# A float32 decoder layer on one core: the order at the joints, the rotary's engine, and where evictions stand

## The chip, the cores and the metric

The kernel runs on one core of a Trainium2 chip. The metric is the device time of one execution in microseconds (us). A core has a matrix engine (TensorE, PE in the rows; PEld is its weight load), VectorE (DVE), ScalarE (ACT), GpSimd (POOL) and SyncE (SP), which here issues the loads. The TensorE clock has two levels, 1.2 and 2.4 GHz; the rows give the granted clock of a stretch as a share of the higher one.

## The reference

One layer on 256 tokens of width 2048, in float32, with an RMS norm before and after each part:

```python
f = swiglu(rmsnorm(x, ffn1_pre_g), ffn1_w_gate, ffn1_w_up, ffn1_w_down)      # 2048 -> 5632 -> 2048
x = x + 0.5 * rmsnorm(f, ffn1_post_g)
proj = rmsnorm(x, mix_pre_g) @ w_in                                          # q, k, v of two groups of 8 heads
o_a = moba_attention(partial_rope(q_a), partial_rope(k_a), v_a)              # rotary on 32 of 128 dimensions
o_b = stick_breaking_attention(q_b, k_b, v_b)
o = concat([rmsnorm(o_a, moba_out_g), rmsnorm(o_b, sb_out_g)])
x = x + rmsnorm(o @ w_out, mix_post_g)
f = swiglu(rmsnorm(x, ffn2_pre_g), ffn2_w_gate, ffn2_w_up, ffn2_w_down)
x = x + 0.5 * rmsnorm(f, ffn2_post_g)
```

With 256 tokens MoBA has one block, so its attention is plain causal softmax.

## The kernel before

The program runs through three parts: FFN 1 (tiles named f1, or f), the mixing part (mix) and FFN 2 (f2). The residual x lies in `xn`, 128 tokens on the partitions, two token tiles t = 0, 1 and four column chunks c of 512.

**Weights.** All weights are streamed from HBM once, in blocks of up to 1 MB, on SP's queue, into three raw buffers (`Weights.RAW`). A block is cut into pieces of 128x1024 numbers. ScalarE casts each piece to a hi part (`whi`, L142), VectorE subtracts that to get the lo part (`wlo`, L147), and TensorE multiplies hi by the activations' hi and lo parts and lo by their hi part, summed in PSUM. `split_next` does the cast and returns the subtraction as a function; `PARTS` = 4 pairs of parts exist beside those that a joint takes from the general slots.

**Block products.** Some pairs of weight rows go through sums (a seven-product scheme: `add_sums` L103 to L111 makes the sums in the raw buffer, in two steps around the casts), the others are plain. `HALVES` and `OUT` give the order of the pairs for w_down and w_out. Each has two column blocks u = 0, 1. Behind the last pair with sums the products are joined (`joins`, L740 to L745), spread over the steps that follow; `later(n, f)` puts f behind the n-th next piece. At the end of a block each bank is added to its row (`finish`, `join` L750), `Post.take` squares it on ScalarE (L388) and multiplies it by the gain row on VectorE (L660).

**Joints.** Where one part ends and the next begins, `Rows.tail` keeps the last three pairs back and runs them bank by bank: `mm(t, c)` is one bank of the tail, in the order (0,0), (0,1), (1,0), (1,1). `handover.end` writes by hand the order of all four compute engines (`ordered`): the bank's sum L750, the square, the gain L660, `column` (the rstd of one tile: L396 and L397 before the last square, L399, L375, L376 and three rounds of L371 and L372 behind it), the update of xn (L651), and `Pre.turn`: TensorE transposes xn (L479), ScalarE writes the hi part of the normed activations xg (L445), VectorE the lo part (L446). `take_over` then multiplies the first four pieces (`AHEAD`) of the next weights for tile 0, turns tile 1 and multiplies them for tile 1. Elsewhere the scheduler of the language sets the order of each engine.

**The mixing part.** `project_qk` makes q and k of two heads at a time. `put_qk` adds the two halves of a product (L632), multiplies by the norm's factor R (L1107), and for the group with rotary shuffles 32 rows (L1110) and does three steps on GpSimd: times the sine table (L1111), times the cosine table (L1112), added (L1113). The scores (`sp`, L1142) come a step or two later. `norm(g, start)` places the norms of the attention's output in the steps of what follows; its last part makes the pairs o0 to o7 for the product with w_out (o0 and o6 with sums, L671 to L677).

## Time and profile before

| | |
|---|---|
| time, median of three runs | 1872.8 us (1872.69 to 1872.9) |
| profiled execution | 1871.75 us, span 1870.0 us |
| TensorE busy | 1828.5 us, 98% of the span |
| VectorE busy | 1573.6 us, 84% |
| ScalarE busy | 1034.5 us, 55% |
| GpSimd busy | 86.7 us, 5% |
| mean granted TensorE clock | 0.992 |
| moved by DMA | 359.91 MB, mean 192 GB/s |

Joint 1 (FFN 1 to the mix) lies at 707 to 747 us, the rotary heads at 898 to 999, joint 2 (mix to FFN 2) at 1111 to 1158, and the last boundary between two column blocks at 1805 to 1823. All times in the rows are counted from the start of the span, of one execution; the seconds of an engine that nobody waits for cost nothing.

### The profile page before, as it was taken

The page shows a single profiled execution, that of the slowest core. Times are in us where ns is not written, and L with a number is a line of the kernel's source. Part 1 is how long each engine was busy: PE and PEld are TensorE (multiplying, and loading weights), DVE is VectorE, ACT ScalarE, POOL GpSimd, SP SyncE. Part 2 cuts the span into 40 slices and gives each one's busy share as a digit, 9 for nine tenths or more (in the row PEclk, how much of TensorE's full clock was granted, in tenths as well). Part 3 has the DMA queues.
Part 4 walks back from the last instruction along what each step waited for, and adds up shares of the span by engine and source line. Part 5 has one row for each costly group of instructions (what it writes and reads, how often), then busy time and mean ns, then how long its engine had stood idle before and what let it go on. Part 6 is the DMA issues. An engine that isn't in the chain of part 4 may idle for free.

```text
span 1870.0 us, 23366 instructions
## 1 busy us (share of the span) xinstructions
PE 1828.5 (98%) x8586; PEld 1519.7 (81%) x8586; DVE 1573.6 (84%) x2181; ACT 1034.5 (55%) x1388; POOL 86.7 (5%) x96
## 2 busy tenths in 40 slices
PE   9999999999999998999989997999999999999997
PEld 8888888888888876888878786788888888888876
DVE  6999998769999988556885786999999668999988
ACT  7655555545565554655545554765555445555553
POOL 0000000000000000000453100000000000000000
PEclk9999999999999999999999998999999999999999
DMA  8466555555655745554445455555555465555753
GB/s 269 150 209 210 200 192 203 185 198 183 210 203 205 259 169 186 187 180 158 158 144 171 170 194 169 169 188 204 201 195 215 175 224 181 199 205 194 252 197 136
DMA packets 181859, 359.91 MB, mean 192 GB/s; under 512 B 8880, under 2 KB 58224, under 8 KB 181744
## 3 DMA queue, kind: packets, MB, share of 16 engines
q1 hardware_dynamic: 179360, 351.31, 54.1%
q0 software_dynamic: 2208, 7.04, 1.1%
q8 instruction: 67, 1.10, 0.2%
q14 instruction: 48, 0.39, 0.1%
q10 hardware_dynamic: 176, 0.07, 0.0%
HBM read 354.19 MB, written 4.19 MB: 192 GB/s over the span
## 4 chain that ended last, share of the span: by engine, by line
PE 86%; DVE 9%; ACT 2%; issue 1%; DMA 1%; POOL 1%; DVEq 0%; ACTq 0%; SPq 0%
PE b L698 36%; PE d L698 17%; PE b_X L698 7%; PE pq L516 5%; PE d_X L698 4%; PE pv L535 4%; DVE wlo L147 3%; PE pq L525 3%; PE p L516 2%; PE w L698 2%; PE p L525 1%; PE ht L958 1%; ACT whi L142 1%; PE w_X L698 1%; ACT sqd L388 1%
## 5 line engine op out<-in xcount | busy, mean ns | idle before, releaser
L142 ACT CAST whi<-raw 128x1024 fp32r<-128x1024 f32 (+1 forms) x833 | 816.5, 1005 | 700.3 <-DVE raw L106 175.7
L147 DVE TENSOR_TENSOR wlo<-raw,whi 128x1024 fp32r<-128x1024 f32 (+1 forms) x833 | 952.0, 1169 | 241.8 <-ACT whi L142 235.8
L698 PE MATMUL b<-whi,x 128*128 128x512 f32 x1200 | 370.0, 389 | 0.0
L698 PEld LDWEIGHTS b<-whi,x 128*128 128x128 f32 x1200 | 225.1, 188 | 46.9
L698 PE MATMUL d<-whi,h 128*128 128x512 f32 x768 | 237.4, 389 | 0.4 <-ACT whi L142 0.4
L698 PE MATMUL b<-wlo,x 128*128 128x512 f32 x600 | 203.3, 389 | 0.2
L698 PEld LDWEIGHTS d<-whi,h 128*128 128x128 f32 x768 | 144.0, 188 | 31.1 <-ACT whi L142 1.3
L698 PE MATMUL b_X<-whi,x 128*128 128x512 f32 x400 | 155.8, 390 | 0.0
L516 PE MATMUL pq<-xg_mix,whi 128*128 128x512 f32 x512 | 133.6, 403 | 0.0
L698 PEld LDWEIGHTS b<-wlo,x 128*128 128x128 f32 x600 | 112.5, 188 | 24.5 <-DVE wlo L147 1.1
L698 PE MATMUL d<-wlo,h 128*128 128x512 f32 x384 | 130.6, 389 | 0.0
L516 PEld LDWEIGHTS pq<-xg_mix,whi 128*128 128x128 f32 x512 | 93.3, 191 | 17.3
L698 PE MATMUL d_X<-whi,h 128*128 128x512 f32 x256 | 99.3, 393 | 0.0
L698 PEld LDWEIGHTS b_X<-whi,x 128*128 128x128 f32 x400 | 75.1, 188 | 16.0 <-DVE x L446 0.4
L698 PEld LDWEIGHTS d<-wlo,h 128*128 128x128 f32 x384 | 72.0, 188 | 15.1
L535 PE MATMUL pv<-whi,xg_mix 128*128 128x512 f32 x256 | 82.7, 395 | 0.6 <-DVE xg_mix L446 0.6
L698 PE MATMUL b_X<-wlo,x 128*128 128x512 f32 x200 | 77.8, 389 | 0.0
L525 PEld LDWEIGHTS pq<-xg_mix,wlo 128*128 128x128 f32 x512 | 70.3, 191 | 5.4
L525 PE MATMUL pq<-xg_mix,wlo 128*128 128x256 f32 x512 | 71.7, 283 | 0.0
L111 DVE TENSOR_TENSOR raw<-raw 128x512 f32<-128x512 f32 x88 | 61.3, 697 | 2.0
L110 DVE TENSOR_TENSOR raw<-raw 128x512 f32<-128x512 f32 x88 | 60.8, 691 | 2.0
L106 DVE TENSOR_TENSOR raw<-raw 128x512 f32<-128x512 f32 x88 | 61.0, 693 | 1.6
(326 smaller groups left out, 2650.5 us busy)
## 6 DMA issues: line engine op xcount, KB each, us to landing
raw<-in_ffn_w_down_dram SPq DMA_DIRECT2D x86, 1024.0 KB, 5.0
raw<-in_ffn_w_up_dram SPq DMA_DIRECT2D x168, 512.0 KB, 4.7
raw<-in_ffn_w_gate_dram SPq DMA_DIRECT2D x167, 512.0 KB, 3.7
raw<-in_w_in_dram SPq DMA_DIRECT2D x48, 1024.0 KB, 5.1
raw<-in_w_out_dram SPq DMA_DIRECT2D x15, 1024.0 KB, 4.9
raw<-in_ffn_w_gate_dram SPq DMA_DIRECT2D x4, 1024.0 KB, 5.5
raw<-in_ffn_w_up_dram SPq DMA_DIRECT2D x4, 1024.0 KB, 5.0
xn<-in_x_dram SPq DMA_DIRECT2D x8, 256.0 KB, 6.2
```

The source lines that it names most:

```text
L106: eng.tensor_sub(q[:, 1], q[:, 3], q[:, 1])
L110: eng.tensor_add(q[:, 3], q[:, 3], q[:, 0])
L111: eng.tensor_sub(q[:, 2], q[:, 2], q[:, 3])
L142: self.nc.scalar.copy(hi, raw)
L147: self.nc.vector.tensor_sub(lo, raw, hi.bitcast(F32))
L388: nc.scalar.activation(d, src, AF.Square, accum_out=self.ss[:, t, c:c + 1])
L516: nc.tensor.matmul(p, wh, x, start=k == 0, stop=False)
L525: nc.tensor.matmul(p[:, :T], lo[:, j, f * P:(f + 1) * P], xs(k)[:, 0, :], start=False, stop=k == KD - 1)
L535: nc.tensor.matmul(ps[c], y, w[:, j, c * CH:(c + 1) * CH], start=first and n == 0, stop=last and n == 2)
L698: nc.tensor.matmul(self.ps[x], y, w, start=m == 1, stop=m == self.n[x])
L958: nc.tensor.transpose(p4[:, 2 * j + t], tg[2 * t + 1][:, k * P:(k + 1) * P], ident)
```

## The change

Five things are edited.

1. In `handover` and `take_over`, the four pieces that come next are no longer split in front of the tail's first sum. Their casts come behind the second sum of tile 0. The four lo parts (`lows`) come one behind the gain multiplication of tile 1's first sum and three in `take_over`. The V products of pieces 1 to 3 with tile 0 that need a lo part are done with tile 1's. The updates of xn in chunks 2 and 3 are moved into `take_over`.
2. The first gate and up weights of FFN 2 are loaded as blocks of both matrices, two pieces a block, in place of one block of half the size for each piece.
3. The rotary's cosine table gets ones in the rows without rotary, both tables are multiplied once by R, and all steps of the rotary are on VectorE.
4. The last column block of w_out takes its pairs in the order 4, 6, 5, 0, 7 in place of 4, 5, 6, 7, 0, and the norm of the rotary group starts a step later.
5. The gain multiplications L660 leave `Post.take`. At the boundary between two column blocks they come with steps 7, 8, 13 and 14 of the next block; in the joints and at the end they have places of their own.

```diff
     cos, sin = np.cos(ang), np.sin(ang)
+    m[:, M_COS:M_COS + T] = 1
     m[:ROT, M_COS:M_COS + T] = np.concatenate([cos, cos])
...
-OUT = ((4, 5, 6, 7, 0), (6, 0), (1, 2, 3))
+OUT = (((4, 5, 6, 7, 0), (4, 6, 5, 0, 7)), (6, 0), (1, 2, 3))
...
             c0 = fp * 2 * P
-            if fp == 0:
+            if fp == 0 and n == 1:
                 plan["gu", n, fp] = []
...
                         ]
+            elif fp == 0:
+                plan["gu", n, fp] = [
+                    (None, 4 * c + 2 * s, i) for c in range(4)
+                    for s, i in enumerate(W.add((wg, wu), 4 * c, 4, c0, 4 * P))
+                ]
             else:
...
-    def take_over(pre, mm, ids):
+    def take_over(pre, first, second, ids):
+
         parts = [W.get(ids[m], 0) for m in range(AHEAD)]
+        lows = pre.lows
         for m in range(AHEAD):
-            mm(m, parts[m], 0)
-        W.split_next()()
+            first(m, parts[m], m == 0)
+        more = W.split_next()
         his, los = pre.turn(0, (1,))
         run_all(his)
+        pre.update(1, 1)
         run_all(los)
+        lows[1]()
         his, los = pre.turn(1, (1,))
         run_all(his)
-        mm(0, parts[0], 1)
+        second(0, parts[0], True)
+        lows[2]()
         run_all(los)
+        pre.update(2, 0)
         pre.update(2, 1)
-        mm(1, parts[1], 1)
-        W.split_next()()
+        second(1, parts[1], False)
+        lows[3]()
+        more()
+        second(2, parts[2], False)
+        his, los = pre.turn(2)
+        run_all(his)
+        more = W.split_next()
+        pre.update(3, 0)
+        run_all(los)
+        second(3, parts[3], False)
         pre.update(3, 1)
-        mm(2, parts[2], 1)
-        pre.group(2)
-        mm(3, parts[3], 1)
+        more()
         slots.give(*W.kept)
...
             ordered()
-            for m in range(AHEAD):
-                W.split_next(slots.take)()
             mm(0, 0)
...
             run_all(before)
+            post.finish()
             mm(0, 1)
             finish(1, 0)
+            lows = [W.split_next(slots.take) for _ in range(AHEAD)]
             post.finish()
...
             pre = make()
+            pre.lows = lows
             pre.update(0, 0)
...
             run_all(before)
+            post.finish()
+            lows[0]()
             run_all(los)
...
             pre.update(0, 1)
-            pre.update(1, 1)
-            pre.update(2, 0)
-            pre.update(3, 0)
         return end
...
             self.late.append(((c, t), lambda: nc.vector.tensor_mul(dst, src, self.rows.chunk(c))))
-            if c < NC - 1:
-                self.finish()
...
                     self.finish(c, t)
+                if self.last:
+                    for n in (7, 8, 13, 14):
+                        later(n, lambda: self.post.finish(1))
...
                 W.split_to(i + 1)
-                if j == 1 and k0 + nk < KD:
+                if j != 0 and (k0 + nk) % 4 == 0 and k0 + nk < KD:
                     mm(m, (hi, lo, 1))
...
             def banks(j):
+                if j is None:
+                    return banks(0) + banks(1)
                 if j not in ps:
...
-    cosv = rots[:ROT, :T]
+    cosv = rots[:, :T]
...
-        def mm(m, part, ts):
-            for t in ts:
-                if t not in pv:
-                    pv[t] = bank(f"pv{g}{half}{t}")
-                for terms in ((0, 1), (2,)):
-                    for j in range(part[2]):
-                        k = ids[m][0] + j
-                        mm_tok([pv[t]], part, j, pre.x(k), t, k == 0, k == KD - 1, terms)
+        def mm(m, part, t, groups=((0, 1), (2,))):
+            if t not in pv:
+                pv[t] = bank(f"pv{g}{half}{t}")
+            for terms in groups:
+                for j in range(part[2]):
+                    k = ids[m][0] + j
+                    mm_tok([pv[t]], part, j, pre.x(k), t, k == 0, k == KD - 1, terms)
+
+        def second(m, part, whole):
+            if not whole:
+                mm(m, part, 0, ((1,),))
+            mm(m, part, 1)
...
             rest = AHEAD
-            take_over(pre, lambda m, part, t: mm(m, part, (t,)), [i for _, i in ids])
+            take_over(pre, lambda m, part, whole: mm(m, part, 0, ((0, 1), (2,)) if whole else ((0,), (2,))), second,
+                      [i for _, i in ids])
         for m in range(rest, len(ids)):
             part = W.get(ids[m][1])
-            mm(m, part, (0,))
+            mm(m, part, 0)
             if rest and m == 5:
                 pre.group(3)
-            mm(m, part, (1,))
+            mm(m, part, 1)
             step()
...
             later(0, pre.spread)
+            later(3, lambda: nc.vector.tensor_mul(cosv, cosv, pre.R))
+            later(4, lambda: nc.vector.tensor_mul(sinv, sinv, pre.R[:ROT]))
         vts[g, half] = slots.take([P, NT, 512], F32, f"vt{g}{half}")
...
             q = qk(g, h)[:, j, :]
-            nc.vector.tensor_mul(q, s, pre.R)
+            nc.vector.tensor_mul(q, s, cosv if g == 0 else pre.R)
             if g == 0:
                 sh = tmp.tile([ROT, T], F32, tag="right", name="sh")
-                nc.vector.stream_shuffle(sh, q[:ROT], swap)
-                nc.gpsimd.tensor_mul(sh, sh, sinv)
-                nc.gpsimd.tensor_mul(q[:ROT], q[:ROT], cosv)
-                nc.gpsimd.tensor_add(q[:ROT], q[:ROT], sh)
+                nc.vector.stream_shuffle(sh, s[:ROT], swap)
+                nc.vector.tensor_mul(sh, sh, sinv)
+                nc.vector.tensor_add(q[:ROT], q[:ROT], sh)
         return run
...
             later(f // (1 + half), outs[4 * half + f])
-    norm(0, 2)
+    norm(0, 3)
...
                 run_all(before)
+                post.finish()
                 if t:
```

**Place 1: VectorE in joint 1.** Names: wlo349 to wlo352 are the lo parts of the four next pieces (V weights of the mix), d111_2 and d111_3 the tail's banks for tile 0, fg_f12 and fg_f13 the output rows. Before, from the tail's third own lo part (wlo348) on:

```order
L147 TENSOR_TENSOR wlo348_5901<-raw136_5864,whi348_5900 128x1024
L147 TENSOR_TENSOR wlo349_5909<-raw137_5888,whi349_5908 128x1024
L147 TENSOR_TENSOR wlo350_5913<-raw137_5888,whi350_5912 128x1024
L147 TENSOR_TENSOR wlo351_5919<-raw138_5898,whi351_5918 128x1024
L147 TENSOR_TENSOR wlo352_5923<-raw138_5898,whi352_5922 128x1024
L750 TENSOR_TENSOR fg_f12_2528<-d111_2_5614,fg_f12_2528 128x512
L660 TENSOR_TENSOR fg_f12_2528<-fg_f12_2528,r_ffn1_post_g1_5179 128x512
L396 TENSOR_REDUCE rs_post_f10_5948<-ssq_post_f1_2530 128x1
L397 TENSOR_SCALAR rs_post_f10_5948<-rs_post_f10_5948 128x1
L750 TENSOR_TENSOR fg_f13_2529<-d111_3_5616,fg_f13_2529 128x512
```

After, from the same row on (the line numbers are those of the changed file: L148 is the lo part, L766 the sum, L678 the gain, L402 to L382 the rstd):

```order
L148 TENSOR_TENSOR wlo348_5901<-raw136_5864,whi348_5900 128x1024
L766 TENSOR_TENSOR fg_f12_2528<-d111_2_5610,fg_f12_2528 128x512
L402 TENSOR_REDUCE rs_post_f10_5927<-ssq_post_f1_2530 128x1
L403 TENSOR_SCALAR rs_post_f10_5927<-rs_post_f10_5927 128x1
L678 TENSOR_TENSOR fg_f12_2528<-fg_f12_2528,r_ffn1_post_g1_5179 128x512
L766 TENSOR_TENSOR fg_f13_2529<-d111_3_5612,fg_f13_2529 128x512
L678 TENSOR_TENSOR fg_f14_5952<-fg_f13_2529,r_ffn1_post_g1_5179 128x512
L405 TENSOR_SCALAR rs_post_f10_5927<-ssq_post_f1_2530,rs_post_f10_5927 128x1
L381 TENSOR_SCALAR rs_post_f10_5927<-rs_post_f10_5927 128x1
L382 TENSOR_SCALAR rs_post_f10_5927<-rs_post_f10_5927 128x1
L377 TENSOR_SCALAR rs_post_f10_5927<-rs_post_f10_5927 128x1
L378 SCALAR_TENSOR_TENSOR rs_post_f10_5927<-rs_post_f10_5927 128x1
```

The four lo parts wlo349 to wlo352 stood between the tail's own lo part and the first sum; now the sum follows at once. And a little further on after the change, from tile 1's first sum (d111_4) on:

```order
L766 TENSOR_TENSOR fg_f12_2528<-d111_4_5618,fg_f12_2528 128x512
L402 TENSOR_REDUCE rs_post_f11_6027<-ssq_post_f1_2530 128x1
L403 TENSOR_SCALAR rs_post_f11_6027<-rs_post_f11_6027 128x1
L678 TENSOR_TENSOR fg_f12_2528<-fg_f12_2528,r_ffn1_post_g1_5179 128x512
L148 TENSOR_TENSOR wlo349_5956<-raw137_5888,whi349_5955 128x1024
L452 SCALAR_TENSOR_TENSOR xg_mix0_5997<-xt_mix00_6014,G_97,xg_mix0_5997 128x128 x2
L452 SCALAR_TENSOR_TENSOR xg_mix1_5998<-xt_mix01_6017,G_97,xg_mix1_5998 128x128 x2
L452 SCALAR_TENSOR_TENSOR xg_mix2_5999<-xt_mix10_6042,G_97,xg_mix2_5999 128x128 x2
L452 SCALAR_TENSOR_TENSOR xg_mix3_6000<-xt_mix11_6045,G_97,xg_mix3_6000 128x128 x2
```

Here one of the four lo parts, wlo349, now stands between the gain of tile 1's first sum and the four lo parts of xg (L452, L446 before); the other three stand behind tile 1's transposes.

**Place 2: VectorE in the rotary, the second pair of heads.** pq0110 and pq0111 are the banks of k of heads 2 and 3, g their sums, qk01 the result that `sp2` and `sp3` need. Before:

```order
L632 TENSOR_TENSOR g_7962<-pq0110_7801,right_7960 128x256
L673 TENSOR_TENSOR or6_7958<-or6_7958 128x128
L1107 TENSOR_TENSOR qk01_7832<-g_7962,R_mix_6359 128x256
L674 TENSOR_TENSOR or6_7958<-or6_7958 128x128
L1110 STREAM_SHUFFLE sh_7965<-qk01_7832 32x256
L147 TENSOR_TENSOR wlo417_7983<-raw171_7849,whi417_7982 128x1024
L632 TENSOR_TENSOR g_7972<-pq0111_7802,right_7970 128x256
L677 TENSOR_TENSOR o6l_8008<-or6_7958,o6h_8007 128x896
L1107 TENSOR_TENSOR qk01_7832<-g_7972,R_mix_6359 128x256
L147 TENSOR_TENSOR wlo418_8012<-raw171_7849,whi418_8011 128x1024
L1110 STREAM_SHUFFLE sh_7975<-qk01_7832 32x256
```

After (L650 is the sum, L1135 the multiplication, L1138 the shuffle, L1139 and L1140 the two steps that were on GpSimd; `rots` holds both tables):

```order
L1135 TENSOR_TENSOR qk01_7830<-g_7958,rots_6077 128x256
L1138 STREAM_SHUFFLE sh_7961<-g_7958 32x256
L148 TENSOR_TENSOR wlo417_7977<-raw171_7845,whi417_7976 128x1024
L1139 TENSOR_TENSOR sh_7961<-sh_7961,rots_6077 32x256
L650 TENSOR_TENSOR g_7967<-pq0111_7800,right_7965 128x256
L1140 TENSOR_TENSOR qk01_7830<-qk01_7830,sh_7961 32x256
L1135 TENSOR_TENSOR qk01_7830<-g_7967,rots_6077 128x256
L1138 STREAM_SHUFFLE sh_7970<-g_7967 32x256
L687 TENSOR_TENSOR or6_7954<-or6_7954 128x128
L1139 TENSOR_TENSOR sh_7970<-sh_7970,rots_6077 32x256
L688 TENSOR_TENSOR or6_7954<-or6_7954 128x128
L1140 TENSOR_TENSOR qk01_7830<-qk01_7830,sh_7970 32x256
```

Two operations follow each shuffle on VectorE, and the shuffle no longer waits for the multiplication but reads the sum g. The last of them for pq0111 now stands ahead of wlo418; before, the shuffle stood behind it, and behind o6l.

**Place 3: VectorE at the last boundary between two column blocks of FFN 2.** fg_f20 and fg_f21 are the rows of the first column block, raw329 (raw325 after) the raw block in which L110 and L111 make the second sums. Before:

```order
L660 TENSOR_TENSOR fg_f21_12028<-fg_f21_12028,r_ffn2_post_g0_14679 128x512
L660 TENSOR_TENSOR fg_f20_12027<-fg_f20_12027,r_ffn2_post_g0_14679 128x512
L750 TENSOR_TENSOR fg_f20_12027<-d210_4_14697,fg_f20_12027 128x512
L750 TENSOR_TENSOR fg_f21_12028<-d210_X_14699,fg_f21_12028 128x512
L147 TENSOR_TENSOR wlo810_15110<-raw329_15005,whi810_15109 128x512
L660 TENSOR_TENSOR fg_f20_12027<-fg_f20_12027,r_ffn2_post_g0_14679 128x512
L660 TENSOR_TENSOR fg_f21_12028<-fg_f21_12028,r_ffn2_post_g0_14679 128x512
L110 TENSOR_TENSOR raw329_15005<-raw329_15005 128x512
L147 TENSOR_TENSOR wlo811_15132<-raw329_15005,whi811_15131 128x1024
L111 TENSOR_TENSOR raw329_15005<-raw329_15005 128x512
```

After (L766 is the sum, L678 the gain, L111 and L112 the second sums):

```order
L766 TENSOR_TENSOR fg_f20_12009<-d210_4_14679,fg_f20_12009 128x512
L766 TENSOR_TENSOR fg_f21_12010<-d210_X_14681,fg_f21_12010 128x512
L148 TENSOR_TENSOR wlo810_15088<-raw325_14987,whi810_15087 128x512
L111 TENSOR_TENSOR raw325_14987<-raw325_14987 128x512
L148 TENSOR_TENSOR wlo811_15110<-raw325_14987,whi811_15109 128x1024
L112 TENSOR_TENSOR raw325_14987<-raw325_14987 128x512
L678 TENSOR_TENSOR fg_f21_12010<-fg_f21_12010,r_ffn2_post_g0_14661 128x512
L678 TENSOR_TENSOR fg_f20_12009<-fg_f20_12009,r_ffn2_post_g0_14661 128x512
L148 TENSOR_TENSOR wlo812_15126<-raw325_14987,whi812_15125 128x1024
```

The four gain multiplications stood two and two ahead of the sums in the raw block; now two stand behind them and the other two some pieces later.

## Rows read from the trace of the kernel before

**Rows 1.** The page: busy time, share of the span and instructions of each engine; and the chain of work that ended last, as shares of the span by engine.

```profile
PE 1828.5 (98%) x8586; PEld 1519.7 (81%) x8586; DVE 1573.6 (84%) x2181; ACT 1034.5 (55%) x1388; POOL 86.7 (5%) x96
...
PE 86%; DVE 9%; ACT 2%; issue 1%; DMA 1%; POOL 1%; DVEq 0%; ACTq 0%; SPq 0%
```

**Rows 2.** Who waited for whom, TensorE alone: what waited and for what, then us in total, how often, and the longest.

```profile
PE xt_f L479 <- DVE xn L651: 8.2, 2, 7.6
PE xt_mix L479 <- DVE xn L651: 6.7, 1, 6.7
PE sp L1142 <- POOL qk L1113: 4.9, 2, 3.3
...
PE pv L535 <- DVE xg_mix L446: 0.6, 1, 0.6
```

**Rows 3.** Windows around joint 1 (first two) and joint 2: start and end, length, then busy us (and instructions) of PE, PEld, DVE, ACT and POOL, the granted clock, the DMA share and GB/s.

```profile
721.00:727.70 6.70, 0.01 (x1) 0.01 (x1) 5.44 (x18) 1.44 (x4) 0.54 (x1) 0.71 0.82 307
727.70:732.80 5.10, 5.10 (x21) 4.28 (x22) 3.77 (x12) 2.90 (x10) 0.54 (x1) 0.71 0.06 10
1126.50:1134.30 7.80, 0.17 (x2) 0.01 (x1) 6.54 (x18) 1.45 (x4) 0.00 (x0) 0.73 0.47 150
1134.30:1140.80 6.50, 6.50 (x21) 5.34 (x22) 4.27 (x13) 2.90 (x10) 1.13 (x2) 0.54 0.23 83
1140.80:1157.50 16.70, 14.06 (x114) 13.36 (x113) 12.79 (x31) 6.93 (x18) 3.24 (x6) 1.00 0.57 180
```

**Rows 4.** Timeline of joint 1: start, length in us, engine, line, operation, output and inputs, shape, number of instructions; in brackets the idle time before and what ended it.

```profile
707.18 0.39 PE L698 MATMUL d<-whi,h 128*128 128x512 f32 x1
...
710.05 3.49 DVE L147 TENSOR_TENSOR wlo<-raw,whi 128x1024 fp32r<-128x1024 f32 x3
...
717.65 2.00 ACT L142 CAST whi<-raw 128x1024 fp32r<-128x1024 f32 x2 [2.65 <-DMA raw<-in_w_in_dram]
...
718.74 2.36 DVE L147 TENSOR_TENSOR wlo<-raw,whi 128x1024 fp32r<-128x1024 f32 x2 [2.29 <-ACT whi L142]
...
723.35 0.68 DVE L750 TENSOR_TENSOR fg_f<-d,fg_f 128x512 f32<-128x512 f32 x1
...
726.89 1.41 DVE L651 SCALAR_TENSOR_TENSOR xn<-fg_f,rs_post_f,xn 128x512 f32<-128x512 f32 x2
...
727.69 1.11 PE L479 MATMUL xt_mix<-ident,xn 128*128 128x128 f32 x4 [6.72 <-DVE xn L651]
```

**Rows 5.** Timeline of joint 2, same columns.

```profile
1115.80 4.62 DVE L147 TENSOR_TENSOR wlo<-raw,whi 128x1024 fp32r<-128x1024 f32 x4
...
1117.07 0.50 PE L698 MATMUL w<-wlo,o 128*128 128x512 f32 x1 [0.90 <-DVE wlo L147]
...
1134.29 1.12 PE L479 MATMUL xt_f<-ident,xn 128*128 128x128 f32 x4 [7.63 <-DVE xn L651]
...
1140.99 0.69 DVE L750 TENSOR_TENSOR fg_mix<-w_X,fg_mix 128x512 f32<-128x512 f32 x1 [0.77 <-PE w_X L698]
...
1145.35 1.32 PE L479 MATMUL xt_f<-ident,xn 128*128 128x128 f32 x8 [0.57 <-DVE xn L651]
...
1148.73 1.34 PE L520 MATMUL p<-xg_f,whi 128*128 128x256 f32 x8 [2.06 <-DVE xg_f L446]
```

**Rows 6.** Timeline of the rotary, the second pair of heads, same columns.

```profile
943.26 0.49 PE L1142 MATMUL sp<-qk 128*128 128x128 f32 x2 [1.65 <-POOL qk L1113]
...
944.73 2.75 POOL L1111 TENSOR_TENSOR sh<-sh,rots 32x256 f32<-32x256 f32 x1 [1.52 <-DVE sh L1110]
...
950.25 0.80 PE L1142 MATMUL sp<-qk 128*128 128x128 f32 x2 [3.29 <-POOL qk L1113]
```

**Rows 7.** Grouped by line. First row: the rotary's first GpSimd step, count, then ns min/median/max, first and last start. Second and third: VectorE from 902 to 990, busy us and mean ns of one, idle time before. Last: the same for the lo parts over the whole run.

```profile
L1111 POOL TENSOR_TENSOR sh<-sh,rots x16: 724/816/4217, 897.9 to 996.1; 32x256 f32<-32x256 f32 x16
...
L147 DVE TENSOR_TENSOR wlo<-raw,whi 128x1024 fp32r<-128x1024 f32 x26 | 35.7, 1372 | 9.7 <-ACT whi L142 7.3 <-PE pq L525 2.4
...
L632 DVE TENSOR_TENSOR g<-pq,right 128x256 f32<-128x256 f32 x12 | 5.0, 413 | 0.3 <-ACT right L630 0.3
...
L147 DVE TENSOR_TENSOR wlo<-raw,whi 128x1024 fp32r<-128x1024 f32 x743 | 894.2, 1228 | 241.8 <-ACT whi L142 235.8 <-PE pq L525 2.4
```

**Rows 8.** Windows, columns as in rows 3: a stretch behind the rotary's longer wait, most of the rotary, the two boundaries between column blocks (FFN 1 and FFN 2), and an undisturbed stretch near the end.

```profile
951.30:956.45 5.15, 5.15 (x18) 4.29 (x17) 2.33 (x8) 1.09 (x2) 0.00 (x0) 0.55 0.54 186
902.00:990.00 88.00, 83.06 (x472) 73.00 (x471) 72.47 (x155) 43.29 (x80) 48.98 (x41) 0.96 0.47 153
...
675.70:686.70 11.00, 10.17 (x43) 7.46 (x42) 9.73 (x13) 5.11 (x6) 0.00 (x0) 1.00 0.43 161
1812.60:1822.50 9.90, 9.07 (x37) 6.53 (x37) 8.63 (x11) 5.17 (x6) 0.00 (x0) 1.00 0.48 182
1842.90:1859.30 16.40, 16.40 (x73) 13.31 (x71) 14.25 (x30) 5.12 (x9) 0.00 (x0) 1.00 0.15 54
```

**Rows 9.** Timeline of the boundary in FFN 2, columns as in rows 4.

```profile
1810.26 1.30 DVE L660 TENSOR_TENSOR fg_f<-fg_f,r_ffn_post_g 128x512 f32<-128x512 f32 x2
...
1813.98 4.41 ACT L142 CAST whi<-raw 128x1024 fp32r<-128x1024 f32 x5 [3.26 <-DVE raw L111]
```

**Rows 10.** Timeline of the first pair of the output norm, columns as in rows 4.

```profile
1062.26 1.09 DVE L677 TENSOR_TENSOR o0l<-or,o0h 128x896 fp32r<-128x896 f32 x1
...
1062.98 0.62 PE L698 MATMUL w<-whi,o0h 128*128 128x512 f32 x2
```

More of the change, by code (lines that the diff above doesn't have):

```diff
@@ L192 @@
 HALVES = (
-    ((0, 2, 1, 4, 3, 6, 5, 7, 8, 9, 10, 11), (2, 4, 6), ()),
-    ((13, 12, 15, 14, 17, 16, 18), (12, 14, 16), (19, 20, 21)),
+    (((0, 2, 1, 4, 3, 6, 5, 7, 8, 9, 10, 11),) * 2, (2, 4, 6), ()),
+    (((13, 12, 15, 14, 17, 16, 18),) * 2, (12, 14, 16), (19, 20, 21)),
 )
 H_SUMS = HALVES[0][1] + HALVES[1][1]
-OUT = ((4, 5, 6, 7, 0), (6, 0), (1, 2, 3))
+OUT = (((4, 5, 6, 7, 0), (4, 6, 5, 0, 7)), (6, 0), (1, 2, 3))
 @with_exitstack
@@ L241, in plan_ffn @@
                     for j, w in ((0, wg), (1, wu)):
-                        step = 2 if (n, c, j) == (1, 0, 0) else 4
+                        step = 2 if (c, j) == (0, 0) else 4
                         plan["gu", n, fp] += [
@@ L267, in plan_rows @@
                 (p, W.add_sums(w, 2 * p, c0) if p in sums else W.add(w, 2 * p, 2, c0, 2 * CH))
-                for p in (pairs if u == 1 else pairs + tail)
+                for p in (pairs[1] if u == 1 else pairs[0] + tail)
             ]
@@ L842, in first_pair @@
                 first = AHEAD
-                take_over(pre, mm, [i for _, _, i in ids])
+                take_over(pre, lambda m, part, _: mm(m, part, 0), lambda m, part, _: mm(m, part, 1), [i for _, _, i in ids])
             else:
```

## Prediction

> **What bounds the kernel now.** I read the page first. TensorE (PE) is busy 98% of the span and carries 86% of the chain of waits [rows 1], so the kernel is bound by PE and by the few places where PE waits or runs at its lower clock. The other engines matter only where PE waits for them. So next comes the list of PE's waits [rows 2], longest first: 8.2 us and 6.7 us for VectorE's update of xn (L651), which are the two joints, and 4.9 us for GpSimd's last rotary step (L1113), twice. Then the windows [rows 3]: around each joint PE is idle for some 7 us and then works on at a granted clock of 0.71 (5.1 us) or 0.54 (6.5 us), where the stretch behind it has 1.00. A stretch of s us at a granted clock c holds s·c of work at full clock, so the loss is 5.1·0.29 = 1.5 us and 6.5·0.46 = 3.0 us. Last the timelines of the joints [rows 4, 5], the rotary [rows 6], with its grouped rows [rows 7] and windows [rows 8], the boundary between column blocks [rows 9] and the output norm [rows 10].
>
> The measurement can tell about 0.2%, 3.7 us, from no change. The profiled execution took 1871.75 us (span 1870.0), 1.05 us less than the median of 1872.8, so the sum is made against 1871.75 and 1.05 is added at the end.
>
> **Joint 1 (first FFN to mix).** Before, VectorE makes the lo parts of four pieces of the next weights before it touches the tail's sums. Two of them wait until 718.74 for ScalarE's casts at 717.65, which wait for a load [rows 4]. The norm of tile 0 begins only behind them, and PE stands 6.72 us before its transposes at 727.69. After, the norm chain stands in front, behind only the tail's own three lo parts (710.05, 3.49 us). The tail's second bank is full after 36 matmuls from 707.18; at 16.40 us for 73 [rows 8] that is 715.3. From the second L750 (723.35) to the transposes (727.69) the chain took 4.34 us, so xn is there at about 719.8 (0.1 for the hand-over). PE itself reaches the transposes after 60 matmuls, at 720.7 to 721.0. It no longer waits there, with about 1 us to spare: 6.7 us go, and with the stop the slow stretch behind it, 1.5 us; so does a 0.6-us wait for xg [rows 2]. Together 8.8 us.
>
> Part comes back. Call T the moment of these transposes. Between T and those of tile 1 PE has the rest of the tail (6.5·0.54 = 3.5 us at full clock [rows 3]) and the first products of four pieces (in joint 2 from 1140.80 to 1145.35 less a wait of 0.57: 4.0 us [rows 5]), 7.5 us. VectorE's chain over the same part took 11.06 us in joint 2 (1134.29 to 1145.35), of which 0.77 was a wait for the slow PE (1140.99) and about 0.5 is what slow transposes delayed. lows[0], which now stands in it, adds 1.15 (3.49/3 per part). So 10.9 against 7.5: PE will stand about 3.3 us, in two pieces (for lows[0] or the xg lo parts, then for xn of tile 1). The three other lows, 1.15 each, then come between the products of tile 1; I put 1.1 us of small waits on them (bounds 0, as PE has 1.4 us or more of products per piece, and 3.4, if all are exposed). New cost 4.4; **gain 4.4**. The loads stand in the same order on SP. The one that waits for the buffer of lows[1] is issued later, as that lo part now comes behind tile 1's transposes; its pieces come after all four kept ones, and I take nothing for it (if it is late, that adds to the third rival).
>
> **Joint 2 (mix to second FFN).** Before: 0.90 us at 1117.07, where the out-projection's joins (four additions) stood ahead of the tail's lo parts; the stop of 7.63; 3.0 at the low clock; 0.57 and 2.06 at tile 1 [rows 5]. That is 14.2. The new pair order of w_out brings those joins one pair earlier, so the 0.90 goes too. The new plan for gate and up puts two pieces into each 1-MB block, so three buffers hold six pieces; four parts no longer need a fourth load. New waits as in joint 1, 4.4. **Gain 9.8.**
>
> **Rotary.** Before, PE waits 1.65 and 3.29 us for GpSimd [rows 6], whose same multiplication takes 724 ns at least and 4217 ns at most [rows 7]; one of 2.75 us lies right in front of the longer wait. Then 5.15 us run at 0.55 [rows 8]: 2.3 us lost. After, two products with tables made once replace the three GpSimd steps; VectorE gets two more 32x256 operations for each of 16 heads' q and k. The trace has none on VectorE. The nearest are the addition L632 (128x256, 413 ns) and, as the upper end, the same multiplication on GpSimd at its minimum, 724; I take 413: 32·0.413 = 13 us over some 90 us, in which VectorE was busy 72.5 of 88 [rows 8]. In the same stretch the lo parts take 1372 ns in place of 1228 over the whole run [rows 7], so 26·0.144 = 3.7 us of VectorE time come back when GpSimd is quiet, and others like it. In the order, the last rotary addition of the waited-for head now stands ahead of one lo part and of the o6l split, which before stood ahead of the shuffle. Both waits should go: 4.9 + 2.3, **gain 7.2** (bounds 0 and 7.2).
>
> On sharing, the Trainium skill's page "SBUF — State Buffer" (section "SBUF: two separate sides") says that a VectorE operation with two SBUF inputs and a GpSimd operation that reads SBUF shut each other out. The trace agrees: the 724 to 4217 ns and the 1372 against 1228.
>
> **Block boundaries.** In both FFNs' last halves, four gain multiplications (L660, 1.30 us for two) stood ahead of the sums L110 and L111 that ScalarE's casts wait for (3.26 us) [rows 9], and PE ran 43 matmuls in 11.00 us and 37 in 9.90. At 0.2247 each that is 9.66 and 8.31: 1.3 and 1.6 us lost [rows 8]. Spread over later steps, they stand behind what PE needs. VectorE is busy 14.25 of 16.40 us near the end [rows 8], so four more of 0.65 fit in. **Gain 2.8.** In the mix the same multiplications move to the tail's steps; I count nothing, for they lie beside the matmuls of a pair; uncovered, four of 0.65 would cost 2.6. At the kernel's end one of them changes places beside ScalarE's squares; uncovered, 0.65 per tile.
>
> **Output norm.** It starts one step later. The first pair's lo part (o0l) ended at 1063.35 and the first product that needs the pair ran at 1062.98 [rows 10]. Now norm and PE both move back by some four matmuls, not quite equally: **−0.4** (bounds 0 and −1.5).
>
> **Sum.** 4.4 + 9.8 + 7.2 + 2.8 − 0.4 = 23.8. 1871.75 − 23.8 + 1.05 = 1849.0 us, 1.3% less.
>
> **Rivals.**
> *The clock falls again.* Stops of 1 to 2 us remain at each joint. Before, 0.57 and 2.06 us left the next stretch at 1.00, and 3.29 us in the rotary was followed by 0.55 [rows 3, 8]. If the new stops work like the latter, each joint loses 2.3 to 3.0: 1852 for one, 1854 for both.
>
> *The rotary makes VectorE the bound.* VectorE is busy 72.5 of 88 us in this stretch, and the pieces before the waits are its fullest. If the net 8 us or more of added work delays lo parts or q, half to all of the 7.2 is lost: 1853 to 1856. Against it: the stalls there came from GpSimd, in rows up to six times its shortest. The skill's page "Perfetto Trace Analysis" (section "Optimizing Scalar/DVE Operations") speaks against this edit: with a saturated VectorE one may offload, even to GpSimd, and not the reverse. It adds that the two share a read port, so offloading between them may not help. By its first half the time would be 1856, by its second 1849; the long GpSimd rows stand for the second.
>
> *The next casts are late.* ScalarE must now cast four pieces (2.0 us for two) between tile 0's squares and the hi parts of xg. The last two need the load that landed at 717.65 [rows 4]; casts end near 721.0, xg's hi parts are wanted near 721.4. If the load comes 3 us later, as it competes with others, every step behind T moves: 3 us per joint, 1852 to 1855.
>
> *It doesn't do it.* If the tail's lo parts or ScalarE's squares held the chain and not the four lo parts, the joints stay and only rotary and boundaries gain: 1863. Against it: the waits named at 718.74.
>
> *Slower.* The clock could stay low behind the many short stops. At 0.54 each microsecond of work costs 0.85 more; 24 us of gain are gone when 28 us of work, 14 per joint, run so. Before it came back within 5.1 and 6.5 us. If it took 20 us of work per joint, the time would be 1849 + 34 = 1883.
>
> **Chances.** Forecast 0.55 (its own range 1844 to 1852), clock 0.15, rotary 0.10, casts 0.10, no effect in the joints 0.05, slower 0.03, better than 1843 0.02 (new waits near none: 1840). The range 1843 to 1857 holds the first four and leaves out little more than 1 in 10. Faster by over 0.2%: 0.95; within it 0.02; slower 0.03.
>
> **What would show it.** In the profile after: no PE wait of over 1 us at the first xn of a joint; PE waits for xn of tile 1 of about 2 us each; no GpSimd releaser for sp and a VectorE lo part back near 1230 ns around 902 to 990; clock 1.00 behind the joints; the boundary windows near 0.225 us per matmul. Wrong if PE's waits move to hi casts or lo parts with the same total, or if the windows behind the joints stay near 0.5.

## The result, and the profile after

| | before | after |
|---|---|---|
| median | 1872.85 us | 1847.11 us (1846.16 to 1847.95) |
| ratio | | 0.9862, 95% interval 0.9845 to 0.9879 |
| span of the profiled execution | 1870.0 us | 1844.4 us |

25.7 us less; the forecast was 23.8 less, 1849.0 with a range of 1843 to 1857. The page after (busy times, and the chain by engine), against [rows 1]:

```profile
PE 1820.8 (99%) x8586; PEld 1512.2 (82%) x8586; DVE 1571.2 (85%) x2215; ACT 1032.7 (56%) x1388; POOL 29.7 (2%) x48
...
PE 89%; DVE 7%; ACT 3%; issue 1%; DMA 0%; DVEq 0%; ACTq 0%
```

GpSimd's busy time falls from 86.7 us (5%) to 29.7 us. VectorE is busy 85% of the span (before 84%), and its share of the chain falls from 9% to 7%. PE's longest waits after, against [rows 2] (what waited for what: us in total, times, longest):

```profile
PE xt_mix L485 <- DVE xn L669: 2.1, 1, 2.1
PE xt_f L485 <- DVE xn L669: 1.9, 1, 1.9
PE p L526 <- DVE xg_f L452: 1.8, 4, 0.9
...
PE pv L541 <- DVE wlo L148: 1.1, 2, 0.8
...
PE w L714 <- ACT o0h L692: 0.5, 1, 0.5
```

The stops of 7.6 and 6.7 us for xn and the 4.9 us for GpSimd are gone; two waits of about 2 us for xn, now of tile 1, stand in the joints. To see where the time went, I compared the start of the same matmul (the n-th of 8586) in both traces along the run. What each stretch gained:

| stretch | forecast | measured |
|---|---|---|
| start, until 14 us | 0 | 0.9 |
| boundary of blocks, FFN 1 | 1.3 | 1.3 |
| joint 1 | 4.4 | 4.4 |
| rotary | 7.2 | 8.1 |
| output norm | −0.4 | −0.5 |
| w_out's second block, behind o0 | 0 | −0.4 |
| w_out's tail and joint 2 | 9.8 | 10.9 (1.3 and 9.6) |
| boundary of blocks, FFN 2 | 1.5 | 1.3 |
| rest | 0 | −0.3 |
| sum | 23.8 | 25.7 |

The start is not touched by the change. In seven of the eight later profiles it gains 0.1 to 0.4 us against the kernel before, in joints_only 0.9, so that 0.9 us is not the change's.

Timeline of joint 1 after (start, length, engine, line, operation; in brackets the idle time), against [rows 4]. The kernel is 2.07 us ahead at the tail's start:

```profile
708.28 0.61 PE L714 MATMUL d<-whi,h 128*128 128x512 f32 x2
...
711.69 0.68 DVE L766 TENSOR_TENSOR fg_f<-d,fg_f 128x512 f32<-128x512 f32 x1
...
714.02 0.68 DVE L766 TENSOR_TENSOR fg_f<-d,fg_f 128x512 f32<-128x512 f32 x1
...
718.98 0.60 PE L485 MATMUL xt_mix<-ident,xn 128*128 128x128 f32 x4
...
721.19 0.16 DVE L402 TENSOR_REDUCE rs_post_f<-ssq_post_f 128x1 f32<-128x3 f32 x1 [1.61 <-ACT sqd L394]
...
722.05 1.22 DVE L148 TENSOR_TENSOR wlo<-raw,whi 128x1024 fp32r<-128x1024 f32 x1
...
723.32 0.50 PE L541 MATMUL pv<-wlo,xg_mix 128*128 128x512 f32 x1 [0.30 <-DVE wlo L148]
...
728.79 1.41 DVE L669 SCALAR_TENSOR_TENSOR xn<-fg_f,rs_post_f,xn 128x512 f32<-128x512 f32 x2
729.59 1.32 PE L485 MATMUL xt_mix<-ident,xn 128*128 128x128 f32 x8 [2.12 <-DVE xn L669]
...
733.04 0.73 PE L541 MATMUL pv<-wlo,xg_mix 128*128 128x512 f32 x2 [0.75 <-DVE wlo L148]
```

The tail's sum (L766) at 711.69 now comes at once behind its own three lo parts; the norm chain is through before PE arrives, and the transposes at 718.98 wait for nothing. On the clock of the kernel before that is 721.05. From there to the transposes of tile 1 it is 10.61 us, on the chain over lows[0] (722.05) and xn (728.79); PE waits 0.30, 2.12 and 0.75.

Windows after (busy us of PE, PEld, DVE, ACT, POOL, then granted clock, DMA, GB/s): up to the joint's transposes, behind them, joint 2, and the two boundaries, against [rows 3, 8]:

```profile
700.00:718.98 18.98, 18.98 (x84) 15.35 (x83) 17.71 (x33) 9.84 (x13) 0.00 (x0) 1.00 0.77 263
718.98:740.50 21.52, 18.34 (x89) 14.29 (x88) 18.91 (x44) 10.61 (x30) 1.08 (x2) 1.00 0.34 103
1111.00:1133.00 22.00, 19.04 (x138) 17.07 (x138) 19.17 (x45) 10.20 (x28) 3.75 (x7) 1.00 0.40 136
673.50:684.50 11.00, 11.00 (x50) 9.13 (x49) 11.00 (x15) 6.11 (x8) 0.00 (x0) 1.00 0.49 187
1786.60:1796.50 9.90, 9.90 (x46) 8.19 (x45) 9.90 (x14) 5.58 (x6) 0.00 (x0) 1.00 0.54 208
```

The granted clock is 1.00 in each. At the two boundaries between column blocks PE runs 50 matmuls in 11.00 us and 46 in 9.90, where it ran 43 and 37.

### The profile page after: what moved, and what is told of

Same layout as the page of the kernel before. It is cut to its first block, busy times and chain, and to the rows that moved or that the text cites. A ratio compares the mean times of both kernels' runs of the same rounds, so it can differ in the third digit from the quotient of the medians.

```text
span 1844.4 us, 23315 instructions
## 1 busy us (share of the span) xinstructions
PE 1820.8 (99%) x8586; PEld 1512.2 (82%) x8586; DVE 1571.2 (85%) x2215; ACT 1032.7 (56%) x1388; POOL 29.7 (2%) x48
## 4 chain that ended last, share of the span: by engine, by line
PE 89%; DVE 7%; ACT 3%; issue 1%; DMA 0%; DVEq 0%; ACTq 0%
PE b L714 37%; PE d L714 18%; PE b_X L714 7%; PE pq L522 6%; PE d_X L714 4%; PE pv L541 3%; PE pq L531 3%; PE w L714 3%; DVE wlo L148 3%; PE p L522 2%; ACT whi L143 1%; PE p L531 1%; PE ht L979 1%; PE w_X L714 1%; ACT sqd L394 1%
## 5 line engine op out<-in xcount | busy, mean ns | idle before, releaser
L148 DVE TENSOR_TENSOR wlo<-raw,whi 128x1024 fp32r<-128x1024 f32 (+1 forms) x833 | 945.7, 1162 | 229.1 <-ACT whi L143 225.4
L112 DVE TENSOR_TENSOR raw<-raw 128x512 f32<-128x512 f32 x88 | 61.0, 694 | 1.9
L111 DVE TENSOR_TENSOR raw<-raw 128x512 f32<-128x512 f32 x88 | 60.6, 689 | 1.9
```

What stands on the lines that cost most here:

```text
L111: eng.tensor_add(q[:, 3], q[:, 3], q[:, 0])
L112: eng.tensor_sub(q[:, 2], q[:, 2], q[:, 3])
L148: self.nc.vector.tensor_sub(lo, raw, hi.bitcast(F32))
```

## Experiments

**rot_only.** The rotary's part alone, in the kernel before: the lines of the diff on `cosv`, `sinv` and `put_qk`.

> The kernel before with the rotary's part of the change alone: tables multiplied once by R, all steps on VectorE. Theory (the parts are independent, and the rotary gave what the traces show at its place, 8 us): 1865 us, both waits of TensorE for GpSimd gone, no slow clock behind them, joints as before. Rival (the rotary gained only because the joint ahead of it had changed, or the joints' gain contains part of it): 1869 or more, with new waits of TensorE for VectorE in the rotary.

Measured 1865.09 us, ratio 0.9959 (0.9944 to 0.9974): 7.7 less. Both waits for GpSimd are gone, and the matmuls behind the rotary are 8.1 us ahead, exactly as in the full change. The part stands alone, and the rival (1869 or more) falls.

**joints_only and plan_only.** The joints' order with its loads, and the loads alone:

```diff
+            elif fp == 0:
+                plan["gu", n, fp] = [
+                    (None, 4 * c + 2 * s, i) for c in range(4)
+                    for s, i in enumerate(W.add((wg, wu), 4 * c, 4, c0, 4 * P))
+                ]
```

> The kernel before with the joints' order and the loads of the second FFN's first pieces as after; rotary, order of w_out's pairs and gain multiplications as before. Theory (4.4 us in joint 1, some 9.5 in joint 2, independent of the rest): 1859 us; TensorE waits about 2 us for xn in each joint; the 0.9-us wait for a lo part in w_out's tail stays. Rival (the joints' gain needs the earlier joins in w_out's tail, or the later start of the gain multiplications): 1863 or more, with a wait of over 3 us at the first xn of joint 2.

> The kernel before with the loads alone: the first gate and up weights of the second FFN as blocks of both matrices, two pieces a block, in the old order of work. Theory (it is the order on VectorE that held the chain, the loads only make the new order possible): 1 to 3 us less than before, 1870 to 1872, with TensorE still standing over 5 us in joint 2 and a slow clock behind. Rival (the fourth piece's load, which waited for a buffer, held joint 2): 6 us less or more, 1867 or below, with the stop in joint 2 under 3 us.

joints_only: 1856.71 us, ratio 0.9915 (0.9901 to 0.9930), 16.0 less; expected were 13.9 less. By the traces 0.9 of it lies at the start, as above; the joints gained 4.7 and 9.6. Its PE waits:

```profile
PE sp L1166 <- POOL qk L1137: 4.8, 2, 3.3
PE xt_mix L484 <- DVE xn L668: 2.1, 1, 2.1
PE xt_f L484 <- DVE xn L668: 1.9, 1, 1.9
...
PE w L715 <- DVE wlo L147: 1.2, 2, 1.0
```

The waits for xn are 2.1 and 1.9 us as in the full change, and the waits for GpSimd and for w_out's lo part are still there. ScalarE's casts and VectorE's lo parts move together in this run; which of the two moves is worth how much is not parted.

plan_only: 1872.12 us, ratio 0.9998 (0.9988 to 1.0007): nothing. Its joint 2:

```profile
1116.44 0.51 PE L703 MATMUL w<-wlo,o 128*128 128x512 f32 x1 [0.93 <-DVE wlo L147]
...
1125.03 2.36 DVE L147 TENSOR_TENSOR wlo<-raw,whi 128x1024 fp32r<-128x1024 f32 x2 [1.36 <-ACT whi L142]
...
1133.99 1.12 PE L484 MATMUL xt_f<-ident,xn 128*128 128x128 f32 x4 [7.96 <-DVE xn L656]
```

PE still stands 7.96 us. The load of the fourth piece is issued at 1117.96 in place of 1120.45, but its block lands at 1123.9 (the casts start then), so the last lo parts are made at 1125.03 where before it was 1125.16 ([rows 5] shows what follows). The loads alone are worth nothing; the gain comes with the order.

**spread_undone.** The gain multiplications at once, as before:

```diff
-                if self.last:
-                    for n in (7, 8, 13, 14):
-                        later(n, lambda: self.post.finish(1))
...
+            if c < 2:
+                self.finish()
```

> The changed kernel with the gain multiplications at the boundary between column blocks made at once, as before; all else as after. Theory (they cost 1.3 us at each of the two FFNs' last boundaries, and nothing in the mix): 1849.7 us, 2.6 more than the changed kernel. Rival (the gain at the boundaries is an accident of where other work lies): 1847, no difference.

Measured 1851.32 us (1850.14 to 1851.58), 4.2 more than the changed kernel. By the traces the FFN boundaries lose 1.3 each, as expected, and w_out's boundary, where I had expected nothing, 1.4. Another 0.8 is lost in joint 2 of the profiled execution, where the granted clock is 0.50 from 1125.5 to 1128.8 (the row stands with the rivals below). PE's waits at w_out's boundary:

```profile
1083.23 0.73 PE L716 MATMUL w<-whi,o6h 128*128 128x512 f32 x2 [0.53 <-ACT whi L143]
1084.17 0.73 PE L716 MATMUL w<-whi,o 128*128 128x512 f32 x2 [0.22 <-ACT whi L143]
```

They wait for casts that wait for L112, as in [rows 9]. The kernel before shows no such loss there; its second block began with two plain pairs, 4 and 5, and the new order puts pair 6, with sums, second. So the spreading is needed for the new order, not only in the FFNs.

**out_undone and norm_early.** Both old orders (`OUT` and `norm(0, 2)`) back in the changed kernel, and only `norm(0, 2)`.

> The changed kernel with w_out's old pair order and the norm of the rotary group at its old step; all else as after. Theory (from the traces: the new order gained 1.3 us in w_out's tail and the later norm lost 0.9): 0.4 us slower than the changed kernel, 1847.5. Rival (the sum of the other parts alone, 7.7 + 16.0 + 4.2 = 27.9 against 25.7 measured, means that this part loses 2 us): 1845.

> The changed kernel with only the norm of the rotary group started at its old step, w_out's new pair order kept. Theory (the later norm alone costs the 0.9 us at the first product with o0): 1846.2, the wait for o0h gone. Rival (with the new pair order the early norm gets in the way of the first block's joins, or the norm's products stand in TensorE's way as much): no difference or slower, 1847 to 1848.

1847.45 us (0.9868, 0.9853 to 0.9883) and 1847.35 us (0.9866, 0.9851 to 0.9880): neither differs from the changed kernel by what can be measured. The sum of the parts, 27.9, was too large for another reason than out_undone's rival: spread_undone's 4.2 holds the 1.4 us that only the new pair order would have lost and the 0.8 of its slow clock, and without them the sum is 25.7.

By its trace out_undone loses the 1.3 us in the tail again and wins 0.9 ahead of it. norm_early parts this 0.9: with the early norm alone 0.5 is won at the output norm, and 0.4 stays lost in w_out's second block, so the later norm costs 0.5 and the new pair order 0.4. At the norm PE then waits for a cast, as long as in the kernel before:

```profile
1052.64 0.50 PE L714 MATMUL w<-whi,o0h 128*128 128x512 f32 x1 [0.84 <-ACT whi L143]
```

In w_out's tail the 0.8-us wait for a lo part is back. chain_shorter's trace, with the new orders, has the same wait:

```profile
1098.92 2.94 ACT L143 CAST whi<-raw 128x1024 fp32r<-128x1024 f32 x3 [4.12 <-DMA raw<-in_w_out_dram]
...
1101.28 0.49 PE L715 MATMUL w<-wlo,o 128*128 128x512 f32 x1 [0.76 <-DVE wlo L148]
```

The tail's casts wait 4.12 us for their load there, and 3.06 in the changed kernel's trace, where they began in time. So the joins are no longer what the tail waits for, but the load is, and that differs by more than 1 us between traces. This part of the change is worth 0.4 us in the changed kernel's trace, and it costs 0.6 in chain_shorter's and 0.4 in gp_idle's.

**gp_idle.** GpSimd works beside VectorE, for nobody:

```diff
                 nc.vector.tensor_add(q[:ROT], q[:ROT], sh)
+                idle = tmp.tile([ROT, 192], F32, tag="idle", name="idle", bufs=1)
+                nc.gpsimd.tensor_mul(idle, q[:ROT, :192], sinv[:, :192])
+                for _ in range(3):
+                    nc.gpsimd.tensor_mul(idle, idle, cosv[:ROT, :192])
```

> The changed kernel with GpSimd kept busy in the rotary: for each of the sixteen results four operations on 32x192 numbers of it, as much as the three it did before, whose result nobody reads. TensorE's, VectorE's and ScalarE's order is that of the changed kernel. Theory A (what cost time was that TensorE's scores waited for GpSimd's own long steps): the time stays at 1847, within 1.5 us, though VectorE's lo parts there may take longer than 1213 ns. Theory B (two engines shutting each other out of memory held VectorE back, and with it TensorE): lo parts back near 1370 ns, VectorE's rotary steps far over 406 ns, waits of TensorE for VectorE in the rotary, 1850 or more.

Measured 1852.78 us (0.9896, 0.9879 to 0.9912), 5.7 more. VectorE by line from 888 to 990 (busy us, mean ns), first with the idle work, then after from 888 to 976:

```profile
L148 DVE TENSOR_TENSOR wlo<-raw,whi 128x1024 fp32r<-128x1024 f32 x31 | 38.4, 1238 | 4.8 <-ACT whi L143 4.7
L1139 DVE TENSOR_TENSOR sh<-sh,rots 32x256 f32<-32x256 f32 x16 | 8.9, 557 | 0.1
L1140 DVE TENSOR_TENSOR qk<-qk,sh 32x256 f32<-32x256 f32 x16 | 8.5, 534 | 0.1
```

```profile
L148 DVE TENSOR_TENSOR wlo<-raw,whi 128x1024 fp32r<-128x1024 f32 x29 | 35.2, 1213 | 8.5 <-ACT whi L143 8.3
...
L1140 DVE TENSOR_TENSOR qk<-qk,sh 32x256 f32<-32x256 f32 x14 | 5.7, 406 | 0.1
L1139 DVE TENSOR_TENSOR sh<-sh,rots 32x256 f32<-32x256 f32 x14 | 5.7, 406 | 0.1
```

and gp_idle's timeline, with the window behind the longest wait:

```profile
903.83 0.37 ACT L648 COPY right<-pq 128x256 f32<-128x256 f32 x1 [1.17 <-POOL acc_b L421]
...
934.93 0.81 DVE L1139 TENSOR_TENSOR sh<-sh,rots 32x256 f32<-32x256 f32 x1
...
938.29 6.46 POOL L1144 TENSOR_TENSOR idle<-idle,rots 32x192 f32<-32x192 f32 x3
...
949.24 0.80 PE L1190 MATMUL pt<-ident,at 128*128 128x128 f32 x3 [2.75 <-DVE at L1184]
```

```profile
949.20:953.00 3.80, 3.76 (x11) 3.06 (x12) 3.80 (x11) 2.56 (x7) 0.00 (x0) 0.55 0.85 274
```

The rotary's steps take 557 and 534 ns in place of 406, one of them 0.81 us; the lo parts only 1238 in place of 1213, not the 1370 that I had put to theory B. Other small operations are longer too (L1075, 636 ns in place of 411). Up to 949 the operations on VectorE take 6.1 us longer in all than the same ones in the changed kernel's trace. GpSimd's steps at 938.29 are stretched likewise, 6.46 us for three. PE then waits 2.75 us for VectorE, in the softmax (L1184), and 3.8 us follow at 0.55. The order of the operations on TensorE, VectorE and ScalarE is that of the changed kernel, so the longer operations are the price of GpSimd at work beside them.

Two things limit this reading. The idle work took 73.4 us of GpSimd, the three steps before 57.5. And one wait is for GpSimd's queue: at 903.83 ScalarE waits 1.17 us for a sum of squares (L421) that stands behind the idle work, and at 915.12 PE waits 0.70 us for a norm factor made from that sum.

Theory A fails in its time. But the scores, which waited for GpSimd before, do not wait here: over the two heads in question (940 to 958 on the clock of the kernel before) gp_idle gains 7.8 us where the changed kernel gains 8.1. What the change gained in the rotary is therefore these waits and the slow clock behind them. The cost of both engines at once arises at other places of the same stretch, 5.9 us from 905 to 990 with the slow clock in it. That sharing SBUF, the memory that the tiles lie in, also stretched GpSimd's own steps in the kernel before (724 to 4217 ns) is the prediction's reading; no run parts it from other causes.

**chain_shorter.** A shorter chain to tile 1, in both joints:

```diff
             pre.update(0, 0)
+            lows[0]()
             pre.update(1, 0)
...
             finish(0, 1)
+            run_all(los)
             before, after = post.column(1)
             run_all(before)
             post.finish()
-            lows[0]()
-            run_all(los)
...
             run_all(his)
-            run_all(los)
             mm(1, 1, (2,))
             finish(1, 1)
-            post.finish()
+            run_all(los)
             run_all(after)
```

The last `post.finish()` follows `pre.update(1, 1)`.

> The changed kernel with a shorter chain to tile 1 in both joints: the first lo part stands between tile 0's two updates of xn, the first four lo parts of xg fill VectorE's wait for tile 1's squares, the last sum comes ahead of the next four, and the last gain multiplication behind the updates. Theory (TensorE's waits of 2.1 and 1.9 us for xn of tile 1 are that chain's length): both fall by 1.5 to 2 us, 1843.5. Rival (TensorE then waits for lo parts of xg or of the weights instead, a place further on): the sum of the waits in the joints stays, 1846 to 1847.

Measured 1842.27 us (1841.57 to 1843.13), ratio to before 0.9840 (0.9825 to 0.9855); 4.8 less than the changed kernel (3.9, when each is set against the kernel before as it was measured beside it, 1871.90 and 1872.85). Joint 1, and the waits:

```profile
718.67 1.22 DVE L148 TENSOR_TENSOR wlo<-raw,whi 128x1024 fp32r<-128x1024 f32 x1
...
721.07 1.12 DVE L452 SCALAR_TENSOR_TENSOR xg_mix<-xt_mix,G,xg_mix 128x128 fp32r<-128x128 f32 x4
...
726.92 1.42 DVE L670 SCALAR_TENSOR_TENSOR xn<-fg_f,rs_post_f,xn 128x512 f32<-128x512 f32 x2
727.73 1.32 PE L485 MATMUL xt_mix<-ident,xn 128*128 128x128 f32 x8 [0.41 <-DVE xn L670]
...
731.18 0.73 PE L541 MATMUL pv<-wlo,xg_mix 128*128 128x512 f32 x2 [0.75 <-DVE wlo L148]
```

```profile
PE xt_f L485 <- DVE xn L670: 0.7, 1, 0.7
...
PE xt_mix L485 <- DVE xn L670: 0.4, 1, 0.4
```

lows[0] (718.67) and the first lo parts of xg (721.07) fill times in which VectorE waited (after, 1.61 us for ScalarE's squares at 721.19). The transposes of tile 1 come 8.3 us behind the first (719.42 to 727.73) in place of 10.6. The waits for xn fall from 2.1 and 1.9 to 0.4 and 0.7; the 0.75 for a lo part behind stays. By the traces each joint gained 2.3 us, a little more than expected; the rival falls. The granted clock stays at 1.00 behind both stops in this profile (719 to 740 and 1110 to 1135).

## Why the prediction was right, and where not

**Joint 1.** Forecast: PE, not the chain, sets T, at 720.7 to 721.0, then 10.9 us to tile 1 and 4.4 us of new waits. Measured 721.05, 10.61 and 3.17 us of waits. That the waits came out 1.2 us smaller and the gain did not grow has two reasons that the forecast lacks. In a steady stretch one matmul starts 0.23 us behind the other though each takes 0.39, so a stop costs 0.16 us more than its idle time, and the next start behind it comes 0.1 late: some 0.8 us for three stops. Another 0.4 is lost at 742.83, for which the trace names no wait. The gain of 4.4 came out, and that these errors cancel to the tenth is luck; joints_only gives it (4.7) without the other parts.

**Joint 2.** 9.8 forecast, 10.9 measured, of which 1.3 in w_out's tail and not in every execution (the load, above). The term mis-sized is the new waits: 4.4 forecast, 2.95 measured (0.87, 1.86, 0.22); none of them is for one of the three later lows, for which 1.1 was put. That the loads were only needed for the order, not worth time, was not said; plan_only shows it.

**Rotary.** Both waits went, and VectorE's two steps cost 406 ns each against the 413 taken. 8.1 in place of 7.2: the loss at the low clock was counted from 951.30 on (2.3 us), but it had begun with the scores at 950.25, and 6.20 us at 0.54 are 2.9. The remaining 0.3 is not traced. The text there says 16 heads' q and k; it is eight heads', sixteen results, and the 32 operations are right. The sharing rule of the Trainium skill ("SBUF — State Buffer", section "SBUF: two separate sides"), by which a VectorE operation with two SBUF inputs and a GpSimd operation that reads SBUF shut each other out, agrees with gp_idle where L1139 and L1140, with two SBUF inputs each, lengthen from 406 to 557 and 534 ns; the lo parts, with two SBUF inputs as well, took 1238 ns in place of 1213, and why they lengthen so little no run shows. The Trainium skill's page "Perfetto Trace Analysis" (section "Optimizing Scalar/DVE Operations") says that offloading from a saturated VectorE, even to GpSimd, may make sense; that it speaks against the reverse, as the forecast has it, is the forecast's own reading, and here the reverse gained 7.7 us (rot_only). Its second half, that the two share an SBUF read port and offloading between them might not help, agrees.

**Boundaries.** 2.8 forecast (its terms, 1.3 and 1.6, add up to 2.9), 2.6 measured. The step that failed is "in the mix I count nothing": spread_undone shows 1.4 us there. It is no gain against the kernel before, since only the new pair order would have brought that loss.

**Norm.** −0.4 forecast, −0.5 measured. The new pair order cost another 0.4 in w_out's second block (norm_early), which the forecast had not.

**The sum.** Without the start's 0.9 the change gained 24.8 against 23.8. The mechanism of each large term is borne out by a run of its own; the joints' new waits were put too large, and the terms above were missing. The signs named for the profile after are all there: no wait at the first xn of a joint, 2.1 and 1.9 us for xn of tile 1, no GpSimd ahead of sp, lo parts at 1213 ns, clock 1.00, boundaries at 0.22 us per matmul.

**The rivals.** The clock did fall again, in part. In the profile after it didn't, but the four executions after lie in two pairs: 1846.16 and 1846.52 us at a mean granted clock of 0.998, 1847.95 and 1847.69 at 0.996 (these two left no trace). In out_undone's profile the transposes of tile 1 in joint 1, behind the same 2.12-us stop, were followed by the first row here; the second is the same window after, the third joint 2 in spread_undone:

```profile
731.00:734.50 3.50, 3.50 (x11) 2.81 (x12) 3.10 (x6) 1.92 (x8) 0.00 (x0) 0.54 0.00 0
...
731.00:734.50 3.50, 2.75 (x12) 1.97 (x11) 3.50 (x8) 1.24 (x5) 0.00 (x0) 1.00 0.15 14
...
1125.50:1128.80 3.30, 3.30 (x15) 3.08 (x16) 2.54 (x6) 2.17 (x8) 1.08 (x2) 0.50 0.43 161
```

Six profiles have these joints: after, joints_only, spread_undone, out_undone, norm_early and gp_idle. Behind tile 1 of joint 1 the clock fell in three of them (out_undone, norm_early, gp_idle), in joint 2 in three (spread_undone, out_undone, gp_idle). It cost less than the rival's 2.3 to 3.0: joint 1 gains 4.1 to 4.3 us with such a fall and 4.4 to 4.7 without, joint 2 8.4 to 8.8 and 9.6. What decides whether it falls, no run shows. The casts were in time (xg's hi parts began at 719.40, 0.4 us behind the transposes). VectorE as the bound, no effect in the joints, and slower did not happen.

## What to carry to other kernels

Put a serial chain that the bound engine waits for ahead of work that only has to be ready later, and check what that work holds: loads, buffers, casts. When a stop shrinks, its price can fall twice, by the stop and by the slow clock behind it: here 6.7 and 1.5 us in joint 1, 7.6 and 3.0 in joint 2. The sentence ahead of the prediction that the seconds of an engine that nobody waits for cost nothing does not hold for GpSimd here: in gp_idle they cost 5.7 us, with VectorE's operations longer beside them.

## What the runs showed of the hardware

GpSimd work whose result no engine reads cost 5.7 us of 1847: small VectorE operations with two SBUF inputs took up to 0.81 us in place of 0.41, and 128x1024 ones 1238 ns in place of 1213. And the same stop of 2.12 us was followed by a granted clock of 1.00 in one trace and of 0.54 over 3.5 us in that of a kernel that is the same up to there; in the six profiles with these joints it fell behind six of the twelve stops of 1.9 to 2.1 us for tile 1.
